# Token norms by sums in four column groups and products with a selector, with a new order of the first stage

## The chip, the cores and the metric

The kernel runs on one core of a Trainium2 chip. The core has five engines that run side by side: TensorE multiplies matrices (PE in the profile, and PEld for its loads of the stationary operand), VectorE (DVE), ScalarE (ACT) and GpSimd (POOL) work elementwise, and SyncE (SP) issues most of the transfers between the chip's main memory and the on-chip memory. Each engine has a queue and takes its instructions in the order of that queue; an instruction that waits holds up all that stand behind it. A matmul writes to tiles in a memory called PSUM.

The metric is the device time in microseconds (us) of one execution, the median of several runs.

## The reference

1024 tokens of 1024 channels go through two layers. Each layer begins with an RMS norm over the channels, scaled and shifted by vectors that come from a vector c (for 256 context tokens in the first layer, from c_ctx):

```python
def rmsnorm(x, g):
    xf = x.astype(jnp.float32)
    y = xf * lax.rsqrt(jnp.mean(xf * xf, axis=-1, keepdims=True) + RMS_EPS)
    return (y * g.astype(jnp.float32)).astype(x.dtype)
...
    for l in range(DEPTH):
        shift, scale, gate = jnp.split(sc @ mod_w[l] + mod_b[l], 3, axis=-1)
        hx = modulate(rmsnorm(x, norm_g[l]), shift[:, None], scale[:, None])
        if ctx_out_needed or l % 2 == 0:
            hc = modulate(rmsnorm(ctx, norm_g[l]), shift_c, scale_c)
        ...
        x = x + gate[:, None] * out_x
    return rmsnorm(x, final_g)
```

The first layer projects h to the parts va, vg, ga, xb and gb. The parts va and vg go through a sigmoid gate and a convolution of 31 taps, xb through a short convolution and a linear recurrence in both directions, and the result is projected back. The recurrence has a decay for each channel that comes from a parameter vector lam:

```python
    log_a = -LRU_C * r * jax.nn.softplus(-p["lam"].astype(jnp.float32))
    a = jnp.exp(log_a)
    bx = jnp.sqrt(-jnp.expm1(2.0 * log_a)) * (i * uf)
```

The second layer projects h to u and g, takes u less its windowed means, multiplies with one weight matrix for each of four groups, gates and projects back.

## The kernel before

All data lie with channels on the 128 partitions and tokens along the free axis, so x is eight tiles of 128 x 1024. A product of two fp32 matrices is made of three matmuls on split operands: each operand is cast to a shorter format (`fp32r`) on ScalarE, and the rest is taken by a subtraction on VectorE or GpSimd (`split`). The names carry `h` and `l` for the two parts (`wh_`, `wl_`, `h0h`, `h0l`); `wr_` is the weight as loaded. A product is three matmuls.

The "folds" multiply two weights of the second layer with each other ahead of their use: group g's weight `gh`/`gl` (from `graw`) with four blocks `wh_wu_g_kp`. Each block gives two accumulations of 12 matmuls, `fold_g_kp_0` and `fold_g_kp_1`, whose results are copied out (`fo`) and stored. Folds 0 and 1 run in the first stage, folds 2 and 3 near the end of the first layer. They fill TensorE while the norms and the modulation are being worked out.

**First stage (some 67 us).** Fourteen matmuls on constants (`warm`) start the span. Then `fold(0)` and `fold(1)` run, and beside them x is loaded, squared on ScalarE and summed over its eight tiles on VectorE (`ssq`, two halves of 512 tokens). What remains is a sum over 128 partitions. `rstd_cols` takes it by four matmuls of one column for each half (`ms_x<-ones,ssq`), a square root (`rc`) and a reciprocal on 128 x 4 numbers, a diagonal matrix `dg` made of them and the identity `idx`, and one plain fp32 matmul of `ones` with `dg` (`roots`), which spreads the factor of each token over all partitions. The modulation of x comes from four blocks of c times `modW`: `modr_b` is 16 matmuls of 32 columns each in four column groups of the array, `modrow_b` their copy on ScalarE, and `modt_b` four tiny matmuls that turn it to a column. VectorE scales x by the factor of its token (`x<-x,a,ms_x`), ScalarE makes `h0h` and VectorE `h0l`. The first projection then starts: xb, vg, va and the gates of the recurrence, with the context (`cx`, `xbc`) between them. Six "gates" (`mod<-mod,cL`, 128 x 1024) reduce rows of `modT` with the activated c_ctx (`cL`) for the context.

`decay_rates` works out the decay's constants `chalf` and `cneg` from lam by some twenty small VectorE instructions between two folds of the first stage.

**What sets the order.** In the first stage the order of matmuls is the order of the code, chained one to the next by `mm`, and the order of loads and stores on SP's queue likewise by `load`; `fold_some(n)` takes n steps of the folds, `store_folds(n)` issues n stores. The instructions of the other engines are put in order by a scheduler that goes by the code's order, by dependences and by explicit `issue_after`. From the first projection on (`chained[0] = False`) a second planner in the same program orders them.

**The second norm** (n1, near 757 to 770 us) is the same `rstd_cols` on two halves, while folds 2 and 3 run on TensorE; its factors scale `x1` (`x<-x,a,ms_n`, 16 instructions), and the split x feeds the quads of the second layer (`qa_v`, `qc_v`, ...).

## Time and profile before

| | us |
|---|---|
| median of 3 runs | 1286.2 (1284.6 to 1286.56) |
| the profiled execution | 1282.57 |
| its span | 1280.8 |
| PE busy | 1261.2 |
| DVE busy | 1136.8 |
| ACT busy | 654.6 |
| POOL busy | 290.2 |

The span runs from the first to the last instruction that the profiler recorded, so 1.8 us of the execution lie around it. A row of a timeline gives the start and the length of an instruction or of a run of like ones, the engine, the line of the code, the operation, the tiles that it writes and reads with their numbers left out, and in brackets the idle time ahead of it with what ended it. The length of a matmul includes its way through the array, so consecutive matmuls overlap: the pace is the distance of their starts.

### The profile page before, as it was taken

The page shows a single profiled execution, that of the slowest core. Times are in us where ns is not written, and L with a number is a line of the kernel's source. Part 1 is how long each engine was busy: PE and PEld are TensorE (multiplying, and loading weights), DVE is VectorE, ACT ScalarE, POOL GpSimd, SP SyncE. Part 2 cuts the span into 40 slices and gives each one's busy share as a digit, 9 for nine tenths or more (in the row PEclk, how much of TensorE's full clock was granted, in tenths as well). Part 3 has the DMA queues.
Part 4 walks back from the last instruction along what each step waited for, and adds up shares of the span by engine and source line. Part 5 has one row for each costly group of instructions (what it writes and reads, how often), then busy time and mean ns, then how long its engine had stood idle before and what let it go on. Part 6 is the DMA issues. An engine that isn't in the chain of part 4 may idle for free.

```text
span 1280.8 us, 16137 instructions
## 1 busy us (share of the span) xinstructions
PE 1261.2 (98%) x5824; PEld 1041.3 (81%) x5824; DVE 1136.8 (89%) x1765; ACT 654.6 (51%) x954; POOL 290.2 (23%) x147
## 2 busy tenths in 40 slices
...
PEclk9999999999999999999999999999999999999998
...
GB/s 373 396 219 50 42 75 41 66 42 75 42 82 42 82 124 135 154 140 83 164 49 288 175 214 180 91 130 151 122 98 134 115 123 132 303 227 286 212 105 132
DMA packets 78847, 182.33 MB, mean 142 GB/s; under 512 B 7728, under 2 KB 23472, under 8 KB 78768
## 3 DMA queue, kind: packets, MB, share of 16 engines
...
## 4 chain that ended last, share of the span: by engine, by line
PE 57%; DVE 24%; DMA 10%; issue 4%; ACT 2%; POOL 2%; SPq 0%; POOLq 0%; DVEq 0%; ACTq 0%
PE wob L553 7%; PE vg L553 5%; PE va L553 5%; DVE conv L553 5%; PE xb L553 4%; PE fold L123 3%; DVE l L553 3%; PE g L553 3%; PE ga L553 2%; PE ga L144 2%; PE ga L145 2%; PE gb L553 2%; PE ga L146 2%; DMA yr_t<-y_t 2%; PE xbc L553 2%
## 5 line engine op out<-in xcount | busy, mean ns | idle before, releaser
L553 DVE SCALAR_TENSOR_TENSOR conv<-u,sm,conv 128x505 f32<-128x505 f32 (+6 forms) x224 | 153.7, 746 | 1.0
L1658 POOL TENSOR_TENSOR o<-x,rr 128x256 f32<-128x256 f32 (+1 forms) x10 | 9.7, 1004 | 445.7 <-ACT rr L1658 443.5
L553 ACT ACTIVATE l<-g,sm 128x512 f32<-128x512 f32 (+1 forms) x96 | 58.7, 619 | 57.8 <-PE g L553 57.0
L103 ACT CAST wq_g<-wr_g 128x512 fp32r<-128x512 f32 x48 | 28.2, 620 | 55.5 <-DVE wr_g L998 23.0
L553 POOL TENSOR_TENSOR l<-l,l 128x1280 f32<-128x1280 f32 x16 | 47.1, 2968 | 25.6 <-DVE conv L553 14.1
L123 PE MATMUL fold<-gh,wh_wu 128*128 128x512 f32 x128 | 51.1, 400 | 1.4 <-ACT wh_wu L103 1.4
L123 PE MATMUL fold<-gh,wl_wu 128*128 128x512 f32 x128 | 50.2, 395 | 0.1
L553 PE MATMUL gb<-h0h,wl_gb 128*128 128x512 f32 x128 | 49.9, 390 | 0.3 <-POOL wl_gb L553 0.3
L123 PE MATMUL fold<-gl,wh_wu 128*128 128x512 f32 x128 | 50.1, 392 | 0.0
L553 PE MATMUL va<-h0h,wl_va 128*128 128x512 f32 x128 | 50.0, 390 | 0.1
L553 PE MATMUL vg<-h0h,wl_vg 128*128 128x512 f32 x128 | 49.9, 390 | 0.0
L553 PE MATMUL gb<-h0h,wh_gb 128*128 128x512 f32 x128 | 49.9, 390 | 0.0
L553 PE MATMUL gb<-h0l,wh_gb 128*128 128x512 f32 x128 | 49.9, 390 | 0.0
L553 PE MATMUL va<-h0l,wh_va 128*128 128x512 f32 x128 | 49.9, 389 | 0.0
L553 PE MATMUL va<-h0h,wh_va 128*128 128x512 f32 x128 | 49.8, 389 | 0.0
L553 PE MATMUL vg<-h0h,wh_vg 128*128 128x512 f32 x128 | 49.8, 389 | 0.0
L553 PE MATMUL wob<-ybl,wh_wob 128*128 128x512 f32 x128 | 49.8, 389 | 0.0
L553 PE MATMUL wob<-ybh,wh_wob 128*128 128x512 f32 x128 | 49.8, 389 | 0.0
L553 PE MATMUL wob<-ybh,wl_wob 128*128 128x512 f32 x128 | 49.8, 389 | 0.0
L553 PE MATMUL vg<-h0l,wh_vg 128*128 128x512 f32 x128 | 49.8, 389 | 0.0
L553 DVE TENSOR_TENSOR_SCAN l<-l,l 128x256 f32<-128x256 f32 (+1 forms) x32 | 48.7, 1521 | 1.1
L553 DVE SCALAR_TENSOR_TENSOR conv<-cL,wsum,conv 128x506 f32<-128x506 f32 (+3 forms) x70 | 48.2, 746 | 0.2
...
## 6 DMA issues: line engine op xcount, KB each, us to landing
...
```

Of the source, the lines that this page charges most:

```text
L103: return (nc.scalar.copy(hi, src), eng.tensor_tensor(out=lo, in0=src, in1=hi.bitcast(F32), op=sub))
L123: m = nc.tensor.matmul(*args, **kw)
L144: mm(ps, hi[:, kc], xh[k][:, cols], start=(k == 0), stop=False)
L145: mm(ps, hi[:, kc], xl[k][:, cols], start=False, stop=False)
L146: mm(ps, lo[:, kc], xh[k][:, cols], start=False, stop=(k == ks - 1))
L553: last[eng] = f(*args, **kw)
L1658: tail[eng] = f(*args, **kw)
```

## The change

The edits go together under four heads.

1. **The norms.** `rstd_cols` is gone, and with it the identity in the first stage. `rstd_pair` takes both halves at once: eight matmuls of 32 output rows and 128 columns, spread over the four column groups of the array, write the sums to one tile of 128 x 256; one square root, one reciprocal, a cast (`hi`) and a subtraction (`lo`) follow on that tile; eight matmuls with a `selector` (zeros, with one row of ones for each group) spread the factors over the partitions.
2. **The first fold.** The first tile of `graw` and the first fold weight are loaded and split in halves, in an order of products that takes the first halves first (`first_terms`).
3. **The order of the first stage.** The loads of `modW` are apart from their products and stand earlier, the products are interleaved with folds in steps (`fold_part` takes a piece of a fold), stores stand later, there is one more buffer for them, the activations of c and c_ctx have other places, and all six gates stand behind the split of the context.
4. **The decay constants** are worked out on GpSimd, but for one reciprocal on VectorE, in the first projection.

```diff
-    def decay_rates():
+    def decay_exp():
         nc.scalar.activation(sa, lam, AF.Abs)
         nc.scalar.activation(sa, sa, AF.Exp, scale=-1.0)
-        nc.vector.tensor_scalar(out=sb, in0=sa, scalar1=2.0, scalar2=None, op0=add)
-        nc.vector.reciprocal(sb, sb)
-        nc.vector.tensor_tensor(out=sz, in0=sa, in1=sb, op=mult)
-        nc.vector.tensor_tensor(out=sb, in0=sz, in1=sz, op=mult)
-        nc.vector.memset(sa, 1.0 / 17.0)
+
+    def decay_rates():
+        scaled = lambda o, x, c, op: on("pool", nc.gpsimd.tensor_scalar, out=o, in0=x, scalar1=c, scalar2=None, op0=op)
+        scaled(sb, sa, 2.0, add)
+        vec(nc.vector.reciprocal, out=sb, in_=sb)
+        gp(out=sz, in0=sa, in1=sb, op=mult)
...
-    def rstd_cols(acc, name, idD, rpool, wn):
-        n = acc.shape[-1]
-        nt = n // P
-        ps, root = banks(f"ms_{name}", wn)
-        r = rpool.tile([P, H // P], F32, tag="rc", name=f"rc_{name}")[:, :nt]
-        for c in range(nt):
-            mm(ps[:, c : c + 1], acc[:, c * P : (c + 1) * P], ones[:, 0:1], start=True, stop=True)
-        nc.scalar.activation(r, ps[:, :nt], AF.Sqrt, bias=eps_r)
-        nc.vector.reciprocal(r, r)
-        t = ttile(f"dg_{name}")[:, :n]
-        nc.vector.tensor_tensor(out=t.rearrange("p (c t) -> p c t", t=P),
-                                in0=idD.unsqueeze(1).to_broadcast([P, nt, P]),
-                                in1=r.unsqueeze(2).to_broadcast([P, nt, P]), op=mult)
-        roots = lambda: mm(root[:, :n], ones, t, start=True, stop=True)
-        if not chained[0]:
-            roots()
-        return root[:, :n], roots
+        return act
+
+
+    def selector(name):
+        sel = tpool.tile([P, H], F32R, tag="t", name=f"sel_{name}")
+        nc.vector.memset(sel.bitcast(F32), 0.0)
+        for e in range(4):
+            nc.vector.memset(sel[32 * e : 32 * e + 1, e * P : (e + 1) * P].bitcast(F32), 1.0)
+        return sel
+
+
+    def rstd_pair(accs, name, sel, ps, root):
+        v = ttile(f"sq_{name}")[:, : 2 * P]
+        pair = tpool.tile([P, H], F32R, tag="t", name=f"hl_{name}")
+        hi, lo = pair[:, : 2 * P], pair[:, 2 * P :]
+        for q in range(2):
+            for e in range(4):
+                c = (2 * e + q) % 4 * P
+                mm(ps[32 * e : 32 * e + 32, q * P : (q + 1) * P], ones[:, :32], accs[e // 2][:, c : c + P],
+                   start=True, stop=True, skip_group_check=True)
+        nc.scalar.activation(v, ps[:, : 2 * P], AF.Sqrt, bias=eps_r)
+        nc.vector.reciprocal(v, v)
+        nc.vector.tensor_copy(out=hi, in_=v)
+        nc.vector.tensor_tensor(out=lo, in0=v, in1=hi.bitcast(F32), op=sub)
+
+        def roots():
+            for e in range(4):
+                for i, x in enumerate((hi, lo)):
+                    mm(root(e), sel[:, e * P : (e + 1) * P], x, start=(i == 0), stop=(i == 1))
+        return roots
...
+            for h in HALF:
+                load(graw[0][:, h], grp[g, 0][:, h])
+                load(wraw[:, h], wu[g, 0][:, h])
+            load(graw[1], grp[g, 1])
+            for h in HALF:
+                for raw, hi, lo in ((graw[0], ghs[0], gls[0]), (wraw, *early)):
+                    split(raw[:, h], hi[:, h], lo[:, h], nc.vector)
+            split(graw[1], ghs[1], gls[1], nc.vector)
...
-        def mod_loads(b, qs):
-            if b not in modr:
-                modr[b] = psum(f"modr_{b}")
-            for q in qs:
-                raw = dtile(f"modw_{b}_{q}") if b < 3 else ctile(f"modw_{b}_{q}", F32)
-                load(raw, modW[b, q])
+        modraw = {}
+
+        def mod_loads(b):
+            for q in range(4):
+                modraw[b, q] = dtile(f"modw_{b}_{q}") if b < 3 else ctile(f"modw_{b}_{q}", F32)
+                load(modraw[b, q], modW[b, q])
+
+        def mod_products(b):
+            modr[b] = psum(f"modr_{b}")
+            for q in range(4):
+                raw = modraw[b, q]
...
-            nc.scalar.activation(cL, cL, AF.Silu)
...
-            rstd(accc, eps_r, "c")
+            with tc.issue_after(rstd(accc, eps_r, "c").ins):
+                nc.scalar.activation(cL, cL, AF.Silu)
...
-        load(idx, ident)
         load(ccv, ccol)
-        nc.scalar.activation(cpad[:, :, 0:2], ccv, AF.Silu)
         load(sm, small)
-        fold_some(2)
-        decay_rates()
+        fold_some(3)
+        for k in range(5, 8):
+            last_square = x_load(k)
+        with tc.issue_after(last_square.ins):
+            silu_c = nc.scalar.activation(cpad[:, :, 0:2], ccv, AF.Silu)
+        with tc.issue_after(silu_c.ins):
+            nc.scalar.activation(a1[:, 0, 0:1], eps_r, AF.Sqrt)
+        mod_loads(0)
         fold_some(1)
-        for k in range(5, 8):
-            x_load(k)
         store_folds(1)
-        fold_some(3)
-        rx = [rstd_cols(acc[h][:, :H], f"x{h}", idx, spool, h) for h in range(2)]
-        mod_loads(0, range(4))
-        for _, roots in rx:
-            roots()
-        rx = [r for r, _ in rx]
+        mod_loads(1)
+        fold_some(1)
+        rx = banks("rx", 0)
+        roots = rstd_pair([acc[h][:, :H] for h in range(2)], "x", sel_x, wide("ms_x"),
+                          lambda e: rx[e // 2][:, (e % 2) * 2 * P : (e % 2 + 1) * 2 * P])
+        fold_some(1)
+        mod_products(0)
         mod_row(0)
+        roots()
         mod_cols(0)
         modulate(0)
         modulate(1)
-        mod_loads(1, range(4))
+        mod_loads(2)
+        fold_some(2)
+        mod_products(1)
         mod_row(1)
-        store_folds(2)
-        fold_some(2)
+        fold_part(1)
         mod_cols(1)
+        fold_some(1)
         modulate(2)
         modulate(3)
+        store_folds(1)
+        mod_loads(3)
         fold_some(1)
-        mod_loads(2, range(4))
+        mod_products(2)
         mod_row(2)
+        fold_part(1)
+        mod_cols(2)
+        fold_some(1)
+        fold_part(2)
         store_folds(1)
-        fold_some(2)
-        mod_cols(2)
-        mod_loads(3, range(4))
+        mod_products(3)
         with tc.issue_after(mod_row(3).ins):
             modulate(4)
         modulate(5)
+        fold_part(1)
+        mod_cols(3)
         fold_some(1)
-        mod_cols(3)
         modulate(6)
         last_low = modulate(7)
         w_xb0 = wload(win[3 * KT], "xb0", nc.vector)
-        store_folds(1)
         fold_some(2)
         with tc.issue_after(last_low[0].ins), tc.issue_after(last_low[1].ins):
             ctx_load(0)
-            squares = ctx_load(1)
+            ctx_load(1)
+        store_folds(2)
         w_vg0 = wload(win[KT], "vg0", nc.vector)
         store_folds(2)
         spread_c()
-        with tc.issue_after(squares.ins):
-            gates(2 * KT, 2 * KT + 2)
         raw_va0 = wpool.tile([P, D], F32, tag="wr", name="wr_va0")
         load(raw_va0, win[0])
         store_folds(1)
@@ -538,8 +599,10 @@
         for _ in first:
             pass
         ctx_split(0)
-        with tc.issue_after(ctx_split(1)[1].ins):
-            gates(2 * KT + 2, 2 * KT + 6)
+        high, low = ctx_split(1)
+        with tc.issue_after(high.ins), tc.issue_after(low.ins):
+            decay_exp()
+            gates(2 * KT, 2 * KT + 6)
...
+    wide_n = wide("rs")
+    with tc.issue_after(squared[0].ins), tc.high_priority(offset=EVAC):
+        nc.scalar.activation(dsh[:, 0:1], eps_r, AF.Sqrt)
+        roots = rstd_pair([nacc[h][:, :H] for h in range(2)], "n1", selector("n1"), banks("ms_n1", 0)[0],
+                          lambda e: wide_n[:, 2 * e * P : 2 * (e + 1) * P])
+    roots()
+    rs = [wide_n[:, h] for h in HALF]
     nc.vector.tensor_tensor(out=dsh, in0=m1[:, 0, KH:KT], in1=m1[:, 0, 0:KH], op=sub)
-    rs = [rstd_cols(nacc[h][:, :H], f"n1{h}", idD, hpool, h)[0] for h in range(2)]
```

Three places show how the order of an engine's instructions moves. The numbers behind a name tell tiles of the same name apart.

ScalarE before, in the middle of the first stage: `modrow` is the copy of a block of the modulation, `wh_wu_2` the cast of fold 1's third weight, `h0h` a split of x, `fo` a fold's copy.

```order
L390 COPY modrow_520<-modr_493 128x512
L411 ACTIVATE h0h_533<-x_227,m_132 128x1024
L411 ACTIVATE h0h_539<-x_231,m_132 128x1024
L390 COPY modrow_568<-modr_543 128x512
L103 CAST wh_wu_2_574<-wr_wu_2_572 128x1024
L302 COPY fo_1_580<-fold_1_0_578 128x4x128
L411 ACTIVATE h0h_605<-x_274,m_132 128x1024
L302 COPY fo_1_580<-fold_1_1_579 128x4x128
L411 ACTIVATE h0h_611<-x_282,m_132 128x1024
L390 COPY modrow_653<-modr_628 128x512
L103 CAST wh_wu_3_658<-wr_wu_3_656 128x1024
L302 COPY fo_2_664<-fold_2_0_662 128x4x128
```

ScalarE now, at the same place:

```order
L440 COPY modrow_505<-modr_488 128x512
L461 ACTIVATE h0h_526<-x_238,m_132 128x1024
L343 COPY fo_1_552<-fold_1_0_550 128x4x128
L461 ACTIVATE h0h_532<-x_242,m_132 128x1024
L440 COPY modrow_583<-modr_566 128x512
L461 ACTIVATE h0h_609<-x_285,m_132 128x1024
L343 COPY fo_1_552<-fold_1_1_551 128x4x128
L461 ACTIVATE h0h_615<-x_293,m_132 128x1024
L440 COPY modrow_651<-modr_634 128x512
L103 CAST wh_wu_2_546<-wr_wu_2_544 128x1024
L103 CAST wh_wu_3_630<-wr_wu_3_628 128x1024
```

The cast of `wh_wu_2` stood behind the second `modrow` and ahead of the second pair of `h0h`; it now stands behind the third `modrow`, and directly ahead of the cast of `wh_wu_3`. The matmuls of `fold_1_2_0`, the first that read it, follow the 16 matmuls of `modr_2` on TensorE in both orders.

VectorE before, from the last sum of the context's squares to the first product of the gated convolution (`u`), with the repeated rows between them left out:

```order
L365 TENSOR_TENSOR ssqc<-ssqc,csq_3_823 128x256
L446 SCALAR_TENSOR_TENSOR mod_16_836,m_132<-mod_16_836,cL 128x1024
L446 SCALAR_TENSOR_TENSOR mod_17_839,m_132<-mod_17_839,cL 128x1024
L204 RECIPROCAL ssqc<-sq_c 128x256
...
L104 TENSOR_TENSOR ctl_812<-cx_810,cth_811 128x1024
L446 SCALAR_TENSOR_TENSOR mod_18_913,m_132<-mod_18_913,cL 128x1024
...
L446 SCALAR_TENSOR_TENSOR mod_21_922,m_132<-mod_21_922,cL 128x1024
L553 SCALAR_TENSOR_TENSOR uc_948<-xb_845,sm,uc_948 128x1022
...
L553 SCALAR_TENSOR_TENSOR l_946,m_132<-l_946,cL 128x1024
L553 TENSOR_TENSOR m_132<-m_132,sm 128x8
L553 TENSOR_TENSOR u_1060<-va_0_1061,sg_0_983 128x512
```

VectorE now:

```order
L410 TENSOR_TENSOR ssqc<-ssqc,csq_3_806 128x256
L208 RECIPROCAL ssqc<-sq_c 128x256
...
L104 TENSOR_TENSOR ctl_795<-cx_793,cth_794 128x1024
L496 SCALAR_TENSOR_TENSOR mod_16_894,m_132<-mod_16_894,cL 128x1024
L496 SCALAR_TENSOR_TENSOR mod_17_897,m_132<-mod_17_897,cL 128x1024
L496 SCALAR_TENSOR_TENSOR mod_18_900,m_132<-mod_18_900,cL 128x1024
...
L496 SCALAR_TENSOR_TENSOR mod_21_909,m_132<-mod_21_909,cL 128x1024
L616 SCALAR_TENSOR_TENSOR uc_935<-xb_823,sm,uc_935 128x1022
...
L616 SCALAR_TENSOR_TENSOR l_933,m_132<-l_933,cL 128x1024
L616 TENSOR_TENSOR m_132<-m_132,sm 128x8
L616 RECIPROCAL sb<-sb 128x16
L616 TENSOR_TENSOR u_1074<-va_0_1075,sg_0_970 128x512
```

The first two gates stood ahead of the reciprocal of the context's norm and now stand behind the context's split, and the reciprocal of the decay constants stands ahead of `u`.

TensorE before, at the second norm: the first of the two groups of column sums for one half (the rows of `ms_n` with `ones` and `n1acc`), and the two products that spread the factors.

```order
L123 MATMUL fold_0_1_6369<-gh_1_6304,wh_wu_0_6310 128x512
L123 MATMUL ms_n_6285<-ones,n1acc_5639 128x1 x4
L123 MATMUL fold_0_1_6369<-gl_1_6305,wh_wu_0_6310 128x512
...
L123 MATMUL ms_n_1_6274<-dg_n_6282,ones 128x512
L123 MATMUL fold_2_1_6433<-gh_0_6298,wl_wu_2_6323 128x512
L123 MATMUL fold_2_1_6433<-gh_0_6298,wh_wu_2_6322 128x512
L123 MATMUL fold_2_1_6433<-gl_0_6299,wh_wu_2_6322 128x512
L123 MATMUL fold_2_1_6433<-gh_0_6298,wl_wu_2_6323 128x512
L123 MATMUL ms_n_6285<-dg_n_6293,ones 128x512
```

TensorE now, the sums and the products with the selector:

```order
L123 MATMUL fold_1_1_6424<-gl_0_6322,wh_wu_1_6339 128x512
L123 MATMUL ms_n_0_6294<-n1acc_5652,ones 32x128 x2
L123 MATMUL ms_n_0_6294<-n1acc_5653,ones 32x128 x2
...
L123 MATMUL fold_3_0_6487<-gh_0_6321,wl_wu_3_6352 128x512
L123 MATMUL fold_3_0_6487<-gh_0_6321,wh_wu_3_6351 128x512
L123 MATMUL rs<-hl_n_6297,sel_n_6288 128x256
L123 MATMUL fold_3_0_6487<-gl_0_6322,wh_wu_3_6351 128x512
L123 MATMUL fold_3_0_6487<-gh_0_6321,wl_wu_3_6352 128x512
L123 MATMUL rs<-hl_n_6297,sel_n_6288 128x256 x7
L123 MATMUL fold_3_0_6487<-gh_1_6327,wh_wu_3_6351 128x512
```

The sums, which the four column groups now share, stand in the second accumulation of the second block instead of the first block (and the start of the second), and the products that spread the factors from the second accumulation of the third block (`fold_2_1`) to the first accumulation of the fourth (`fold_3_0`).

75 lines of the change are left out of this document (51 added, 24 removed).

## The prediction

> **What bounds the kernel now.** I read the page first, then TensorE's waits, then the timelines of the first 130 us and of the second norm. The page:
>
> ```profile
> span 1280.8 us, 16137 instructions
> ...
> PE 1261.2 (98%) x5824; PEld 1041.3 (81%) x5824; DVE 1136.8 (89%) x1765; ACT 654.6 (51%) x954; POOL 290.2 (23%) x147
> ...
> PEclk9999999999999999999999999999999999999998
> ```
>
> TensorE is busy in 98% of the span and its clock is granted nearly in full everywhere. So the time can move in two ways only: TensorE gets fewer or cheaper matmuls, or it waits more or less. TensorE's waits, us in total, times and longest:
>
> ```profile
> PE fold L123 <- ACT wh_wu L103: 1.4, 1, 1.4
> ...
> PE gb L553 <- POOL wl_gb L553: 0.3, 1, 0.3
> ```
>
> Asked for 8 to 130 us alone, this view has no row. A first stage without waits has nothing to give but its own matmuls, and whatever is made late there shows at once. The rest of the change must be costed by what it takes from or adds to TensorE's queue, and by the waits that it makes.
>
> **The norms on TensorE.** The first stage, TensorE's timeline (start, length):
>
> ```profile
> 7.05 0.58 PE L123 MATMUL fold<-gh,wh_wu 128*128 128x512 f32 x1
> 7.46 0.40 PE L123 MATMUL fold<-gl,wh_wu 128*128 128x512 f32 x1
> 7.98 0.50 PE L123 MATMUL fold<-gh,wl_wu 128*128 128x512 f32 x1
> ...
> 35.18 1.84 PE L123 MATMUL ms_x<-ones,ssq 128*128 128x1 f32 x16
> 36.95 1.93 PE L123 MATMUL modr<-modw,cpad 128*32 128x256 f32 x32
> 38.81 2.20 PE L123 MATMUL ms_x<-dg_x,ones 128*128 128x512 f32 x4
> 40.85 0.95 PE L123 MATMUL modt<-sm,modrow 128*128 128x2 f32 x8
> ...
> 52.44 0.50 PE L123 MATMUL fold<-gh,wh_wu 128*128 128x512 f32 x1
> 52.77 0.40 PE L123 MATMUL fold<-gl,wh_wu 128*128 128x512 f32 x1
> ```
>
> and the same engine in the chain of work that ended last (start, length, count):
>
> ```profile
> 61.83 5.61 PE fold L123 x24
> 67.44 8.16 PE xb L123 x36
> ...
> 89.67 2.89 PE xbc L553 x24
> ```
>
> By the distance of starts, the old sums of x cost 36.95 - 35.18 = 1.77 us and the old products 40.85 - 38.81 = 2.04, together 3.8. A plain fp32 matmul is two records here. The trace has no sums in four column groups, but `modr` is a product in four groups: 32 records of 256 columns take 38.81 - 36.95 = 1.86, so 0.058 each. The new sums are 16 records of 128 columns. At half of 0.058 they cost 0.46; at the pace of the old one-column records (1.77 / 16 = 0.11) they would cost 1.77, no gain. I take 0.7, near the low end, because `modr` has the same shape of operand, plus what a change of shape costs: behind `modr` the first fold's matmul takes 52.77 - 52.44 = 0.33 instead of the folds' pace of 5.61 / 24 = 0.23, so 0.1 on each side. The new products are eight of 256 columns, as `xbc` has them at 2.89 / 24 = 0.12: together 0.95. So a norm costs 1.65 instead of 3.8 and TensorE is spared 2.1 us (1.0 to 2.4), in each of two norms. The Trainium skill, page "TensorEngine Tiling (Array Packing)", section "Tiling Modes", speaks against this: a change of the tiling mode drains the array. Taken as one whole matmul lost (0.39) on each side of the sums, the norm's gain would be 1.5 instead of 2.1; the 0.33 behind `modr` shows about 0.1 a switch, so I keep 2.1.
>
> **The first fold.** The matmul at 7.98 came 0.52 after its predecessor and not 0.23: it waited for the rest of the first weight. With halves that wait goes, 0.3 us. The start at 7.05 stays, since the warm-up matmuls end just ahead of it. Gain 0.3 (0 to 0.5).
>
> **The first stage's new waits.** ScalarE's timeline there:
>
> ```profile
> 46.12 0.56 ACT L390 COPY modrow<-modr 128x512 f32<-128x512 f32 x1
> 46.58 1.04 ACT L103 CAST wh_wu<-wr_wu 128x1024 fp32r<-128x1024 f32 x1
> ...
> 50.70 1.15 ACT L411 ACTIVATE h0h<-x,m 128x1024 fp32r<-128x1024 f32 x1 [2.59 <-DVE x L408]
> ...
> 53.28 0.57 ACT L390 COPY modrow<-modr 128x512 f32<-128x512 f32 x1
> 53.74 1.05 ACT L103 CAST wh_wu<-wr_wu 128x1024 fp32r<-128x1024 f32 x1
> ```
>
> The cast at 46.58 is that of `wh_wu_2`; its first reader is the fold's matmul at 52.44, six us later, and nothing waits. In the new order this cast stands behind the third `modrow`, which waits for the last matmul of `modr_2`; the fold that reads it stands directly behind `modr_2` on TensorE. So TensorE must wait from the end of `modr_2` for the copy and the cast: 53.74 - 53.28 = 0.46 until the cast begins, 1.05 for the cast, and some 0.25 for two handovers, 1.75 in all. Two matmuls on (0.46) stands the first reader of `wl_wu_2`, which VectorE subtracts only after the cast:
>
> ```profile
> 62.38 1.22 DVE L104 TENSOR_TENSOR wl_xb<-wr_xb,wh_xb 128x1024 fp32r<-128x1024 f32 x1
> ```
>
> 1.22 less 0.46 is another 0.75. The fourth `h0h` (1.15) stands ahead of that `modrow` and may push it by up to 0.6. New wait: 2.5 us (2.3 to 3.1), certain by the order alone. SP's queue is held too: the load of `wr_xb0` waits for this `wl_wu_2`, and the context's tiles and `wr_vg0` stand behind it.
>
> Two smaller waits come with it. The sums now stand two accumulations (24 matmuls, 5.5 us) earlier against the last squares of x, some 0.25. The products wait for the chain square root, reciprocal, cast, subtraction on 128 x 256, against two shorter ones on 128 x 4 before; its dearest part is the reciprocal, whose row is that of the context's norm:
>
> ```profile
> 76.97 1.75 DVE L204 RECIPROCAL ssqc<-sq_c 128x256 f32<-128x256 f32 x1
> ```
>
> With 0.45 for the root, 1.75, and about 0.4 each for cast and subtraction (a third to a half of a 1.22) the chain takes 3.2 with handovers, and twelve matmuls and `modr_0` (2.75 + 1.86 = 4.6) stand between sums and products. ScalarE has the last squares and two table loads ahead of the root, so I leave 0.5 for it (0 to 1). First stage: -2.1 - 0.3 + 2.5 + 0.25 + 0.5 = +0.8. From that I take 0.5 because the pieces of modulation stand up to 2 us earlier and their small waits ahead of `modt` go with it: **+0.3** (-0.8 to +1.7). No load was removed but the identity; what moves is their order, and cover for a late load is thin: `h0h_7` now stands behind the cast of `wh_vg0`.
>
> **Gates and decay constants.** VectorE around 90 us, and TensorE behind it:
>
> ```profile
> 89.41 1.22 DVE L446 SCALAR_TENSOR_TENSOR mod<-mod,cL 128x1024 f32<-128x1024 f32 x1
> ...
> 91.72 3.92 DVE L553 SCALAR_TENSOR_TENSOR uc<-xb,sm,uc 128x1022 f32<-128x1022 f32 x3 [1.08 <-ACT uc L553]
> ...
> 105.51 1.27 DVE L553 TENSOR_TENSOR u<-va,sg 128x512 f32<-128x512 f32 x2
> ```
>
> ```profile
> 107.62 0.40 PE L553 MATMUL g<-uh,wh_gw 128*128 128x512 f32 x1
> ```
>
> Two gates that stood ahead of the reciprocal, where VectorE waited for the context's root, now stand behind the context's split: 2 x 1.2 = 2.4 more ahead of `uc`, of which its wait of 1.08 takes a part. So `uc`, and with it `u`, comes 1.3 later, and the reciprocal of the decay's constants, waiting for GpSimd behind `wl_gw`, adds 0.2 to 0.7. The first of the two `u` ends at 105.51 + 0.64 = 106.15 now, and at 107.6 to 108.1 then. The second `g` needs the PSUM tile that this `u` reads free, at 107.62 (+0.3). I take **+0.3** (0 to 1). Further on the delay is absorbed: VectorE's waits from 85 to 320 us are
>
> ```profile
> DVE uc L553 <- ACT uc L553: 5.7, 9, 1.1
> DVE u L553 <- PE va L553: 2.9, 4, 0.9
> ```
>
> 8.6 us, all on results that follow TensorE's own pace. The 22 small instructions taken from VectorE in the first stage hid under folds and give nothing. On GpSimd 25 of them now stand between the end of `wl_gw`, 121.99 - 16.43 = 105.56, and `wl_vg`, which TensorE reads first at 124.86:
>
> ```profile
> 121.99 2.41 POOL L553 TENSOR_TENSOR wl_vg<-wr_vg,wh_vg 128x1024 fp32r<-128x1024 f32 x1 [16.43 <-ACT wh_vg L553]
> ```
>
> ```profile
> 124.86 0.39 PE L553 MATMUL vg<-h0h,wl_vg 128*128 128x512 f32 x1
> ```
>
> The prices of GpSimd's nearest rows (total, then mean ns of one):
>
> ```profile
> L1658 POOL TENSOR_TENSOR o<-x,rr 128x256 f32<-128x256 f32 x6 | 4.2, 724 | 3.4 <-issue 2.2 <-ACT rr L1658 1.2
> L1507 POOL MEMSET vp<- 128x64 f32 x4 | 0.6, 152 | 0.0
> ```
>
> At 0.152 they take 4 us, at 0.724 18 us; they have 16 columns, so I take the low row, and they end near 112, in the idle 16.43 us. "GPSIMD Engine Reference" of the Trainium skill (section "Key points") adds that GpSimd shares its interfaces to on-chip memory with VectorE, which would slow the convolution beside them; at 4 us of small instructions that would be a few tenths on an engine with the slack above. Cost 0.
>
> **The second norm.** TensorE, then VectorE:
>
> ```profile
> 757.58 0.95 PE L123 MATMUL ms_n<-ones,n1acc 128*128 128x1 f32 x8
> 768.75 1.02 PE L123 MATMUL ms_n<-dg_n,ones 128*128 128x512 f32 x2
> ```
>
> ```profile
> 769.81 10.62 DVE L1376 SCALAR_TENSOR_TENSOR x<-x,a,ms_n 128x512 f32<-128x512 f32 x16 [2.24 <-PE ms_n L123]
> ...
> 785.48 0.69 DVE L997 TENSOR_TENSOR ws_v<-wr_v,wr_v 128x512 f32<-128x512 f32 x1 [0.40 <-DMA wr_v<-wfold]
> ...
> 803.97 0.70 DVE L104 TENSOR_TENSOR x_t1l<-x,x_t1h 128x512 fp32r<-128x512 f32 x1
> ```
>
> ```profile
> 804.75 0.39 PE L1018 MATMUL qc_v<-x_t1h,wq_v 128*128 128x512 f32 x1
> ```
>
> TensorE saves about 2.1 here too (the sums for the other half and the other product have rows of the same lengths). But the first product moves 14 matmuls on (3.2 us of folds, less what TensorE gains), and the first scaling needs the last of eight products instead of the first of two: I put it at 771.6 instead of 769.81. VectorE then has no idle time to 804 but the 0.40 at 785.48, so its splits come 1.4 later, while TensorE comes to them 2.1 earlier. The last `x_t1l` is done at 804.67 and read by the matmul behind the one at 804.75, so there is about 0.1 to spare. TensorE waits there and at the next splits, and what is left of 2.1 is 2.1 - 1.5 = 0.6: **-0.6** (-2.1 to +1.4, the lower end if VectorE starts no later than now, the upper if its whole delay reaches TensorE).
>
> **The sum.** +0.3 + 0.3 - 0.6 = 0.0. The profiled execution took 1282.57 and stays there; it lies 3.6 below the median of the runs, 1286.2. I predict 1286 for the median, no change. A measurement of this kernel tells about 0.2% (2.6 us) from no change.
>
> **The rivals.**
> - *Both norms keep their gain.* Products with the selector arrive at VectorE by 769.8, and in the first stage the 0.5 and 0.25 of small waits don't show: -2.1 - 0.3 + 2.5 - 0.5 = -0.4, gates 0, n1 -2.1, and squares and loads that no longer collide give up to 1 more: -3.5, 1282.7. For it: sums and products are sure to be cheaper, and VectorE has 2.24 idle ahead of the scaling. Against it: the order of the products.
> - *The held queue makes the first projection wait* (the other sign). `wr_xb0`, the context and `wr_vg0` are issued only once `wl_wu_2` is done, near 53.4; `wh_vg0` stands ahead of `h0h_7` on ScalarE, and `h0h_7` is read 21 matmuls after the first projection starts. With 0.4 to 1 us to spare there, a landing of `wr_vg0` more than 1 us later than I place it decides; 3 us late gives +2 here, with the +1.7 of the first stage +3.7: 1290. Against it: the first reader of `wr_vg0` on TensorE comes only after `xb`, 11 us behind its start at 67.44.
> - *GpSimd's small instructions are dear.* They may take 14 us before `wl_vg` at 121.99 is pushed and TensorE's first reader (124.86) with it, that is 0.57 each. At 0.724 they take 18: +3.5, 1289.7. Against it: the 0.152 row.
> - *The column groups don't overlap*, the sums cost 1.77 as before in both norms: +2.1, and the sums' delay of about 1 reaches VectorE in n1: 1289.
>
> **The numbers.** No change 0.37, both norms keep their gain 0.32, the held queue 0.17, column groups 0.09, GpSimd 0.05. Thus faster 0.32, within 0.2% 0.37, slower 0.31. The likeliest case alone spans 1283.6 to 1288.8. The bounds of the terms add up to -2.9 and +4.1, and with the two larger rivals the range is 1281 to 1291.
>
> **What would show it.** TensorE's waits should have a new row, `fold` on ScalarE's `wh_wu` or VectorE's `wl_wu`, of 2 to 3 us near 50; if it is missing, the first stage's sum is wrong. `ms_x` in four groups should take less than 1 us. `xb` should start between 66.7 and 69 (now 67.4). VectorE's `x<-x,a,rs` should start near 771.6 on the old clock, and TensorE should wait for `x_t1l` or `x_t2l` near 804. GpSimd's last small instruction should end ahead of 116. A wait on `h0h`, `wl_vg` or `g` of more than 1 us would make the prediction wrong upward.

## The result: 0.4% slower

| | before | after |
|---|---|---|
| median, us | 1285.79 (4 runs) | 1292.23 (4 runs, 1291.76 to 1292.71) |
| ratio, 95% interval | | 1.0043 (1.0026 to 1.0060) |
| profiled execution, us | 1282.57 | 1291.87 |
| its span, us | 1280.8 | 1289.8 |

1286.0 was predicted, with a range of 1281 to 1291. The ratio is +5.5 us (3.3 to 7.7); it is not the quotient of the two medians, which lie 6.4 us apart. The two traced executions lie 9.3 apart, since that of before took 3.2 less than its median: of the differences between the two traces below, some 3 us do not belong to the change. The page after:

```profile
span 1289.8 us, 16163 instructions
...
PE 1263.5 (98%) x5832; PEld 1039.7 (81%) x5832; DVE 1139.0 (88%) x1750; ACT 654.7 (51%) x955; POOL 297.0 (23%) x173
...
PEclk9899999999999999999999999999999999999998
```

TensorE's clock, full before in every slice but the last, is down in the second one (32 to 64 us). Before, TensorE had no wait from 8 to 130 us. Its waits from 0 to 130 us now (total, times, longest; `warm` was there before, too):

```profile
PE fold L123 <- ACT wh_wu L103: 2.0, 1, 2.0
PE xbc L616 <- POOL wl_xb L616: 1.6, 1, 1.6
PE warm L123 <- DVE ones L161: 1.1, 1, 1.1
PE va L616 <- POOL wl_va L616: 0.7, 1, 0.7
PE fold L123 <- DVE gl L104: 0.5, 1, 0.5
PE fold L123 <- DVE wl_wu L104: 0.5, 1, 0.5
PE ms_x L123 <- DVE ssq L410: 0.2, 1, 0.2
```

The table locates the loss: it gives the start of the first matmul of a few products on TensorE (us), from the timelines of before, of a second trace of the same kernel, of the changed kernel, and of the main experiments, which are told below. `qa_woa` ends the first layer, `qa_v` and `qa_g` are the first products of two groups of the second (the time from one to the other is called the v group), and `fin_ms` belongs to the last norm.

| | `xb` | `g` | `qa_woa` | `qa_v` | `qa_g` | `fin_ms` |
|---|---|---|---|---|---|---|
| before | 67.3 | 106.6 | 671.7 | 800.0 | 812.4 | 1256.2 |
| before, second trace | 67.4 | 106.7 | 671.9 | 800.8 | 813.4 | 1257.6 |
| after | 72.6 | 114.3 | 679.5 | 805.7 | 822.1 | 1265.2 |
| filler | 68.8 | 110.6 | 675.8 | 804.2 | 820.8 | 1266.1 |
| weights early | 66.2 | 108.0 | 673.1 | 800.5 | 816.3 | 1260.2 |
| gate behind | 69.8 | 109.7 | 674.7 | 802.5 | 818.2 | 1264.4 |
| both | 65.3 | 105.2 | 670.3 | 797.8 | 815.4 | 1258.5 |
| both, old second norm | 66.1 | 106.0 | 671.0 | 800.0 | 812.5 | 1258.1 |
| the same, old first fold | 65.3 | 105.2 | 670.2 | 798.7 | 813.9 | 1259.7 |
| new second norm alone | 67.4 | 106.7 | 672.0 | 799.3 | 815.0 | 1260.9 |

After is 5.3 us late at `xb`, 7.7 at `g`, and 7.8 at `qa_woa`: nothing happens between 115 and 670 us. At `qa_v` it is 5.7 late, so the second norm gives 2 us; at `qa_g` it is 9.7 late again: the v group takes 16.4 us instead of 12.4. Three places are to be explained.

**First stage.** TensorE's timeline after:

```profile
33.07 0.41 PE L123 MATMUL ms_x<-ssq,ones 128*32 128x128 f32 x4
33.67 0.63 PE L123 MATMUL ms_x<-ssq,ones 128*32 128x128 f32 x12 [0.19 <-DVE ssq L410]
...
39.06 1.21 PE L123 MATMUL rx<-hl_x,sel_x 128*128 128x256 f32 x8
...
53.64 0.50 PE L123 MATMUL fold<-gh,wh_wu 128*128 128x512 f32 x1 [2.05 <-ACT wh_wu L103]
...
54.90 0.79 PE L123 MATMUL fold<-gh,wl_wu 128*128 128x512 f32 x1 [0.53 <-DVE wl_wu L104]
55.49 1.70 PE L123 MATMUL modt<-sm,modrow 128*128 128x2 f32 x8
...
57.62 0.63 PE L123 MATMUL fold<-gl,wh_wu 128*128 128x512 f32 x1
58.05 0.63 PE L123 MATMUL fold<-gh,wl_wu 128*128 128x512 f32 x1
```

The sums and products are about as cheap as forecast, and the wait on `wh_wu_2` and `wl_wu_2` stands where the prediction put it: 2.05 + 0.53 = 2.6 us. But behind it the folds take 0.63 each at a distance of 0.43, not 0.39 and 0.23. The view by stretches shows why (stretch, length, busy time of PE, PEld, DVE, ACT, POOL, then the clock granted to TensorE, the transfers' share and GB/s). After:

```profile
54.00:56.00 2.00, 1.47 (x7) 1.00 (x5) 0.84 (x1) 1.05 (x1) 0.00 (x0) 0.71 0.43 144
56.00:58.00 2.00, 2.00 (x8) 1.86 (x9) 0.74 (x5) 0.00 (x0) 0.00 (x0) 0.50 0.77 262
58.00:60.00 2.00, 2.00 (x6) 1.56 (x5) 2.00 (x4) 0.00 (x0) 0.00 (x0) 0.50 0.96 278
60.00:62.00 2.00, 2.00 (x6) 1.56 (x6) 1.55 (x2) 0.58 (x1) 0.00 (x0) 0.58 0.94 290
```

Before, at the same place:

```profile
56.00:58.00 2.00, 2.00 (x35) 1.09 (x34) 1.75 (x7) 0.07 (x1) 0.00 (x0) 1.00 1.07 385
```

For some 6.5 us, 55 to 61.5, TensorE runs at half its clock. That is worth about 2.9 us: 0.20 more for each of eleven fold matmuls, and 1.70 for `modt` instead of 0.95. The Trainium skill, "TensorE: Matmul & The Clock Gate", Part 1, describes such a gate, with a window of 3.4 us of idleness ahead of the half clock. The measurement differs from the page: a wait of 2.05 us and one of 0.53, with two matmuls between, were enough here.

The trace of before has such a place too, at its very end. With waits of 0.92 us (up to 1266.95) and 1.76 (up to 1271.88) its clock is 0.55 from 1270 to 1272 and 0.50 after, and the second of two like products takes 1.19 instead of 0.68. TensorE's timeline before:

```profile
1269.03 0.68 PE L1658 MATMUL fin_ms<-dg,ones 128*128 128x256 f32 x2
1271.88 1.19 PE L1658 MATMUL fin_ms<-dg,ones 128*128 128x256 f32 x2 [1.76 <-DVE dg L1658]
```

**Gates.** VectorE's timeline after:

```profile
95.51 1.22 DVE L496 SCALAR_TENSOR_TENSOR mod<-mod,cL 128x1024 f32<-128x1024 f32 x1
...
96.66 3.40 DVE L496 SCALAR_TENSOR_TENSOR mod<-mod,cL 128x1024 f32<-128x1024 f32 x1
...
100.00 3.91 DVE L616 SCALAR_TENSOR_TENSOR uc<-xb,sm,uc 128x1022 f32<-128x1022 f32 x3
```

GpSimd's, after:

```profile
95.97 3.01 POOL L616 TENSOR_TENSOR wl_va<-wr_va,wh_va 128x1024 fp32r<-128x1024 f32 x1 [95.53 <-ACT wh_va L616]
108.19 3.36 POOL L616 TENSOR_TENSOR wl_xb<-wr_xb,wh_xb 128x1024 fp32r<-128x1024 f32 x1 [9.21 <-ACT wh_xb L616]
...
113.75 0.26 POOL L616 TENSOR_SCALAR sb<-sa 128x16 f32<-128x16 f32 x1
114.39 0.22 POOL L616 TENSOR_TENSOR sz<-sa,sb 128x16 f32<-128x16 f32 x1 [0.37 <-DVE sb L616]
```

The sixth gate takes 3.40 us instead of 1.22, while GpSimd subtracts `wl_va` (3.01). The trace of before already had such a pair a little later, a VectorE product over the gate's shape, beside `wl_xb` on GpSimd:

```profile
100.99 3.41 DVE L553 SCALAR_TENSOR_TENSOR l<-l,cL 128x1024 f32<-128x1024 f32 x1
```

```profile
99.92 3.41 POOL L553 TENSOR_TENSOR wl_xb<-wr_xb,wh_xb 128x1024 fp32r<-128x1024 f32 x1 [6.85 <-ACT wh_xb L553]
```

The lengths fit with two engines that take turns: `wl_va` ends at 98.98 and the gate that began at 96.66 ends 1.08 later; `l` of before ends 1.07 behind `wl_xb`. No run tests that by itself.

So `uc` starts at 100.00 (91.72 before), which is 27.4 us behind the start of `xb` instead of 24.4, and ScalarE, whose queue holds the cast of `uc` ahead of that of the weight `wh_xb`, brings the weight late: TensorE waits 1.6 for `wl_xb`. The small instructions of the decay constants cost 0.1 to 0.3 each (one 0.65), and TensorE waits for none of them.

**Second norm.** VectorE's timeline after:

```profile
773.29 1.75 DVE L230 RECIPROCAL sq_n<-sq_n 128x256 f32<-128x256 f32 x1
775.62 1.22 DVE L104 TENSOR_TENSOR gl<-graw,gh 128x1024 fp32r<-128x1024 f32 x1 [0.58 <-ACT gh L103]
776.76 0.28 DVE L231 CAST hl_n<-sq_n 128x256 fp32r<-128x256 f32 x1
777.08 0.43 DVE L232 TENSOR_TENSOR hl_n<-sq_n,hl_n 128x256 fp32r<-128x256 f32 x1
780.08 10.62 DVE L1447 SCALAR_TENSOR_TENSOR x<-x,a,rs 128x512 f32<-128x512 f32 x16 [2.57 <-PE rs L123]
```

The scaling stands 2.4 us later against `qa_woa` than before (100.6 us behind its start, 98.1 before and 98.8 in the second trace of before), for the products of the selector: VectorE has the chain done at 777.5 and then waits for TensorE's turn.

### The profile page after: what moved, and what is told of

It is laid out like the page before. It is cut to its first block, busy times and chain, and to the rows that moved or that the text cites. A ratio compares the mean times of both kernels' runs of the same rounds, so it can differ in the third digit from the quotient of the medians.

```text
span 1289.8 us, 16163 instructions
## 1 busy us (share of the span) xinstructions
PE 1263.5 (98%) x5832; PEld 1039.7 (81%) x5832; DVE 1139.0 (88%) x1750; ACT 654.7 (51%) x955; POOL 297.0 (23%) x173
## 4 chain that ended last, share of the span: by engine, by line
PE 59%; DVE 21%; DMA 12%; issue 3%; POOL 2%; ACT 2%; SPq 0%; POOLq 0%; DVEq 0%; ACTq 0%
PE wob L616 7%; DVE conv L616 5%; PE xb L616 4%; PE va L616 4%; PE vg L616 4%; DVE l L616 3%; PE g L616 3%; DMA wr_wu<-wu 2%; DMA modw<-modW 2%; PE ga L616 2%; PE ga L145 2%; PE ga L144 2%; PE gb L616 2%; PE ga L146 2%; PE qb_v L1084 2%
```

## The experiments

"Late" and "early" are against the kernel before unless another is named. Each but the filler, which ran once, has its ratio to runs of the kernel before on the same chip.

### The first stage

*Weight earlier.* One load moved, so that `wu_1_2` is fetched ahead of the third block of `modW`:

```diff
         roots()
+        fold_some(2)
         mod_loads(2)
-        fold_some(2)
```

> The changed kernel with one edit: fold 1's third weight is loaded ahead of the four modW loads of block 2, so that its cast stands behind the second modrow again. Theory (the wait for this cast, 2.05 + 0.53 us, and the half clock that follows it, some 2.9 us, make the 5.35 us by which xb starts late): both waits go, the folds behind them run at 0.23 us and not 0.43, xb starts at 67.3 to 67.8 instead of 72.79, and the time falls by 5.4 us, to 1286.8. Rival (TensorE waits there anyway, for modW or the next weight, which now land later): xb starts at 70 or later and the time falls by 2.5 us at most.

1290.89 us, ratio 1.0062 (1.0040 to 1.0083), `xb` at 71.3. The wait on `wh_wu_2` went, but two of 1.0 came in its place (`modt` on `modrow`, near 54, and a fold on `wl_wu`, near 66), and the clock was down again from 54 to 58 us, to 0.61 and 0.54. It missed because it made another hole at the same place.

*Filler.* Nine matmuls of `ones` with itself into a tile that nobody reads, ahead of the fold that waits. They lie inside the wait, which stays.

```diff
         mod_products(2)
+        filler = psum("filler")
+        for _ in range(9):
+            mm(filler[:, :P], ones, ones, start=True, stop=True)
         mod_row(2)
```

> The changed kernel with nine plain matmuls of ones (128 columns) put between modr_2 and the fold that waits for the cast; their result is not used. They fill the wait of 2.05 us with work and shorten nothing. Theory (the half clock is a consequence of TensorE standing idle): the clock of 0.50 from 56 to 60 us is gone, the folds behind run at 0.23 us, and xb starts near 69.9, 2.9 earlier than in the changed kernel though the cast comes no earlier. Rival (the low clock has another cause, the load of the chip at this time): the clock falls all the same and xb starts at 72.8 or later.

The stretch that ran at half clock:

```profile
56.00:58.00 2.00, 2.00 (x10) 1.66 (x9) 2.00 (x5) 0.25 (x1) 0.00 (x0) 1.00 0.83 252
```

The clock is 1.00 throughout, and `xb` starts at 68.8 instead of 72.6, `g` at 110.6 instead of 114.3. The fold that waits for the cast starts 20.6 us behind the first sum of the norm, as in after, so nothing but the clock was changed: the half clock is what the idle TensorE brought on itself.

What it costs can be read from four kernels with this first stage, from the first sum of the norm to `xb`. It takes 39.6 us in after and in the run with the old second norm (told below), whose clock is down for 6.8 us by the trace's record; 38.0 in the run with one gate behind (below), where the same two waits leave the clock down for 3.4 us; and 36.3 with the filler. So the fall cost half of its length, 3.2 us in after, and how long it lasts was not the same from run to run. The time of the single filler run, 1292.49, does not show the gain: `fin_ms` is at 1266.1, and the gain has gone behind 675 us.

*Both weights early.* The loads of `wu_1_2` and `wu_1_3` ahead of the third and fourth block, and the fourth `h0h` behind `modrow_2` on ScalarE:

```diff
+        fold_some(2)
         mod_loads(2)
-        fold_some(2)
...
         modulate(2)
-        modulate(3)
         store_folds(1)
-        mod_loads(3)
         fold_some(1)
+        mod_loads(3)
         mod_products(2)
-        mod_row(2)
+        with tc.issue_after(mod_row(2).ins):
+            modulate(3)
```

> The changed kernel with the third and the fourth weight of fold 1 loaded ahead of the modW loads of their blocks, and the third modrow ahead of the fourth h0h on ScalarE, so that neither cast nor that modrow stands behind something TensorE must finish first. Theory (each cast that stands behind a modrow makes TensorE wait, and the pauses bring the half clock): no wait of TensorE over 0.6 us between 8 and 70 us, the clock stays at 1.00, xb starts at 66.8 to 67.8, and the time falls by 5.0 us from the changed kernel's. Rival (the rest of the new order cannot be fed by the transfers): the wait appears once more at another tile, xb starts at 69 or later.

1287.89, ratio 1.0020 (1.0004 to 1.0036). The waits on `wh_wu` and `wl_wu` are gone, the clock is full in this stage, and `xb` starts at 66.2, 1.1 earlier than in the kernel before. From the first sum to `xb` it takes 33.5 us, 2.8 less than with the filler: that is the price of the waits themselves. Against before the loss falls from 5.5 us to 2.6, where 0.5 was expected; the two intervals (3.3 to 7.7 and 0.5 to 4.6) overlap, so it is the traces that show this gain. The norm's saving on TensorE is seen to be real in this stage.

### The gates

*Two gates back* ahead of the context's reciprocal, with the activation of `cL`:

```diff
             load(cL, cc[0].partition_broadcast(P))
+            nc.scalar.activation(cL, cL, AF.Silu)
...
-            with tc.issue_after(rstd(accc, eps_r, "c").ins):
-                nc.scalar.activation(cL, cL, AF.Silu)
+            rstd(accc, eps_r, "c")
...
+        with tc.issue_after(squares.ins):
+            gates(2 * KT, 2 * KT + 2)
...
-            gates(2 * KT, 2 * KT + 6)
+            gates(2 * KT + 2, 2 * KT + 6)
```

> The changed kernel with two of the six gates, and the activation of c_ctx that they need, back where they stood before. Theory (the two gates make uc 2.4 us late, behind it stands the cast of the next xb weight on ScalarE, and TensorE waits 1.6 us for wl_xb and 0.7 for wl_va): both waits go, the first g follows the start of xb by 39.1 us as before (41.7 in the changed kernel), and the time falls by 2.3 us. Rival (the lateness of VectorE comes from the late start of the first projection or from the decay constants): the waits stay and the time is within 0.7 us of the changed kernel's.

1296.87, ratio 1.0088 (1.0062 to 1.0114). The wait on `wl_xb` went, but in the changed order of the first stage the gates delay the context's norm (`ms_c` waits 2.7 for `ssqc`). Besides the fall near 60 us the clock fell to 0.50 at 14 to 16 us, behind the first fold's wait for its second halves. Undoing a part in its old place can cost more than the part.

*One gate behind.* The sixth gate stands behind the subtraction `ul`, where VectorE no longer holds up `uc`:

```diff
-            gates(2 * KT, 2 * KT + 6)
+            gates(2 * KT, 2 * KT + 5)
...
-            vec(nc.vector.tensor_tensor, out=ul, ...)
+            ulop = vec(nc.vector.tensor_tensor, out=ul, ...)
...
             if state is None:
+                with tc.issue_after(ulop.ins):
+                    gates(2 * KT + 5, 2 * KT + 6)
```

> The changed kernel with the sixth gate moved from ahead of uc to behind ul. Theory (this gate runs while GpSimd subtracts wl_va, and both read two operands from the on-chip memory: it took 3.40 us instead of 1.22, and held uc, uh, the cast of wh_xb and with it wl_xb): five gates end before wl_va starts, uc starts 3 us earlier against the start of vg (12.9 us behind it, now 15.8), the waits for wl_xb (1.6) and wl_va (0.7) go, and the time falls by 2.3 us. Rival (uc collides with wl_va instead, or the sixth gate collides with wl_xb and holds u): the first g comes less than 1 us earlier, and the time falls by less than 1.

VectorE's timeline there:

```profile
102.31 1.22 DVE L496 SCALAR_TENSOR_TENSOR mod<-mod,cL 128x1024 f32<-128x1024 f32 x1
...
103.46 3.41 DVE L616 SCALAR_TENSOR_TENSOR l<-l,cL 128x1024 f32<-128x1024 f32 x1
```

1290.95, ratio 1.0045 (1.0030 to 1.0060). The gate takes 1.22 again, and it is `l`, which now runs beside `wl_xb`, that takes 3.41, as before the change. The wait on `wl_xb` is gone. From `xb` to `g` it takes 39.9 us: 39.3 in the kernel before and in the run with the new second norm alone, 41.7 to 41.8 in all runs with the changed gates but for the gates put back, 39.9 in all with the sixth gate behind. So the late gate cost 1.8 at `g`, and 0.6 stays, which fits the wait on `wl_va` (0.7). The time shows none of it: 2.3 us less were expected, and the ratio is that of the changed kernel. That `xb` stands 2.8 ahead of after's is not the gate's doing: the norm's sums came 1.3 earlier, and the clock was down for half as long.

*Both*, weights early and gate behind:

> The edits of the two kernels above together. If the theories hold, all that the changed kernel loses in the first 130 us is regained (xb at 67.3, first g at 105.5 to 106.5), and what is left is the gain of the second norm: 1 to 2 us faster than the kernel before. If the second norm's gain is lost behind it, the time is that of the kernel before within 1 us.

1287.91, ratio 1.0020 (1.0005 to 1.0035). `xb` is 2.0 and `g` 1.4 earlier than before, more than the theory had, and `qa_v` 2.2 earlier; but `qa_g` is 3.0 late, and instead of 1 to 2 us faster the kernel is 2.6 slower than before. What is left is behind the second norm.

### The second norm

*Old norm.* The changed kernel with the second norm of before:

```diff
-    wide_n = wide("rs")
-    with tc.issue_after(squared[0].ins), tc.high_priority(offset=EVAC):
-        nc.scalar.activation(dsh[:, 0:1], eps_r, AF.Sqrt)
-        roots = rstd_pair([nacc[h][:, :H] for h in range(2)], "n1", ...)
-    roots()
-    rs = [wide_n[:, h] for h in HALF]
+    rs = [rstd_cols(nacc[h][:, :H], f"n1{h}", idD, hpool, h)[0] for h in range(2)]
```

> The changed kernel with the second norm as before (column sums for each half, diagonal matrices). Theory (the new second norm gives TensorE 2.0 us at first and takes 3.9 back, since VectorE starts the scaling 2.5 us later than the shift of the stage): the v products begin 2.0 later than in the changed kernel, the waits for qb_v and wq_g (0.9 and 1.1) go, and the time falls by 1.9 us. Rival (what is lost behind the second norm comes from loads that arrive late whatever the norm): the waits stay and the time rises by 2.0 us.

1291.14, ratio 1.0062 (1.0038 to 1.0085). `qa_v` comes later (809.4), `qa_g` where it was (822.1): the norm's gain on TensorE had bought nothing. The waits for `qb_v` and `wq_g` are gone, as expected, but the time did not fall by 1.9; it lies above the changed kernel's, by less than the runs can tell.

*New norm alone* in the kernel before, the same lines the other way round:

> The kernel before with the new second norm (n1) alone: sums by four column groups, selector's products, the Sqrt table ahead; nothing of the first stage or of the gates is changed. Theory: TensorE starts the v group 2 us earlier but the scaling starts about 2.5 us later, so the v group takes 15 to 17 us instead of 12.5 and the time is 0.5 to 2.5 us above before. Rival A: the norm's saving on TensorE is kept, 2 us below before. Rival B: both cancel, within 0.5 us of before.

1287.33, ratio 1.0023 (1.0012 to 1.0035), so +3.0 us. VectorE's timeline:

```profile
765.32 1.75 DVE L225 RECIPROCAL sq_n<-sq_n 128x256 f32<-128x256 f32 x1
767.88 1.22 DVE L104 TENSOR_TENSOR gl<-graw,gh 128x1024 fp32r<-128x1024 f32 x1 [0.82 <-ACT gh L103]
...
773.67 1.41 DVE L1412 SCALAR_TENSOR_TENSOR x<-x,a,rs 128x512 f32<-128x512 f32 x2 [3.90 <-PE rs L123]
```

The sums stand later too. TensorE's timeline before, and then with the new norm alone:

```profile
760.34 0.95 PE L123 MATMUL ms_n<-ones,n1acc 128*128 128x1 f32 x8
```

```profile
762.71 0.64 PE L123 MATMUL ms_n<-n1acc,ones 128*32 128x128 f32 x16
```

The scaling starts 3.9 us later than before (769.81). It is the place of the products in TensorE's queue that decides: VectorE has the chain done at 769.8 and waits 3.90 for them. ScalarE's first cast for the v group, `x_b11h`, comes 3.2 later than its 779.37 too. TensorE's largest wait in the v group, 1.1 us at `qa_g`, is for ScalarE's cast of `wq_g`, which stands behind `x_t4h`, and that waits for VectorE. ScalarE's timeline before, and then with the new norm alone:

```profile
811.20 0.62 ACT L103 CAST x_t4h<-x 128x512 fp32r<-128x512 f32 x1 [4.98 <-DVE x L966]
```

```profile
813.81 0.62 ACT L103 CAST x_t4h<-x 128x512 fp32r<-128x512 f32 x1 [5.12 <-DVE x L995]
814.33 0.61 ACT L103 CAST wq_g<-wr_g 128x512 fp32r<-128x512 f32 x1
```

*Fixes with the old norm.* Both fixes, and the second norm of before:

> The changed kernel with the two weight loads of the first stage ahead of the modulation blocks, the sixth gate behind the `ul` subtraction, and the second norm (n1) as the kernel before computes it; the first norm, the first fold's halves and the decay constants stay as changed. Theory (three separate costs: late weight, late gates, and a scaling that starts later behind the new second norm): the first projection still starts 2.0 us earlier than before, the first product of `g` 1.4 earlier, and with the old norm the v group takes its 12.5 us again, so the time is 1283 to 1285 where before gives 1285. Rival A (the loss behind 675 us is a matter of how the loads fall and not of the norm): the v group still takes 15 us or more and the time is 1287 to 1288, as with both fixes alone.

1285.23, ratio 1.0006 (0.9993 to 1.0018). The v group takes its 12.5 us again and the time is that of before. `xb` and `g` start 1.2 and 0.5 earlier than before, not 2.0 and 1.4, and that does not show in the time.

*Old first fold.* The same, with the loads and the order of the first fold of before:

> As the kernel with the two fixes and the old second norm, with the first fold of the kernel before: whole loads and splits of its inputs and the old order of its first 48 matmuls. Theory (the halves cost, because the second halves land 0.4 us too late for the new order): the square sums of the first norm start up to 0.6 us earlier and the time falls by 0.3 to 0.6 us against the kernel with halves. Rival (the halves gain 0.3 us as the prediction had it): 0.3 us later.

1283.87, ratio 0.9998 (0.9983 to 1.0013). The times alone do not separate it from the kernel with halves, but the traces do. With halves and early weights `xb` starts at 66.2, 65.3, 66.1 and 66.0 in four kernels, without at 65.3, 65.1, 65.2 and 65.4. The halves cost some 0.6 us instead of gaining 0.3. The first fold starts up to 1 us earlier with them (5.6 to 6.3 against 6.6 to 6.9 in these kernels) and gives that back in waits for the second halves, as in the trace of after, TensorE's timeline:

```profile
10.13 0.73 PE L123 MATMUL fold<-gh,wh_wu 128*128 128x512 f32 x2
11.39 0.50 PE L123 MATMUL fold<-gl,wh_wu 128*128 128x512 f32 x1 [0.53 <-DVE gl L104]
```

The sums of the norm then start about when they do without halves, but with halves they wait for `ssq` and take 1.16 us to the next fold, without 0.58: there the 0.6 arises.

One reading stands against the late scaling as the only cause. In the trace of this kernel, with the old norm and the scaling only 98.3 us behind `qa_woa`, the v group takes 15.2 us as well, with two waits on `x_t1l` (2.1 in all); its `x_b11h` comes 110.4 behind `qa_woa`, 107.7 before. So one trace's v group is not the norm's doing alone.

*Delay, too small.* On top of the fixes with the old norm, a reciprocal, a copy and a product on a tile of ones on VectorE ahead of the scaling:

```diff
+    more = ttile("more")[:, : 2 * P]
+    nc.vector.memset(more, 1.0)
+    for _ in range(1):
+        nc.vector.reciprocal(more, more)
+        nc.vector.tensor_copy(out=more, in_=more)
+        nc.vector.tensor_tensor(out=more, in0=more, in1=more, op=mult)
```

> As the kernel with the two fixes and the old second norm, with three more VectorE instructions on a tile of ones between the old norm's diagonal products and the scaling of x: a reciprocal, a copy and a product of 128x256, which is what the new norm puts there (1.75, 0.28 and 0.43 us, together 2.5 us). Nothing else is changed. Theory (VectorE is full from 770 to 829 us and TensorE waits for its scaled x): the v group becomes 2 to 2.5 us longer and so does the time. Rival (the delay is hidden, and what costs is the new norm's order of the scaling or its PSUM banks): the v group stays at 12.5 us and the time does not change by more than 0.5 us.

1284.63, ratio 1.0012 (0.9995 to 1.0029), like the kernel without it. It settled nothing: the three ran in time in which VectorE would have waited, and the scaling started at 769.75.

*Delay, held.* The same with three reciprocals, on the kernel with the old first fold, and a product of the scale `a1` with ones at the end, so that the scaling cannot pass it:

```diff
+    for _ in range(1):
+        nc.vector.reciprocal(more, more)
+        nc.vector.reciprocal(more, more)
+        nc.vector.reciprocal(more, more)
...
+    nc.vector.tensor_tensor(out=a1[:, 0, :], in0=a1[:, 0, :], in1=more[:, :KT], op=mult)
```

> The two fixes, the first fold of before and the old second norm, with three reciprocals, a copy and a product of 128x256 on a tile of ones and a product of the scale by ones in VectorE's queue right ahead of the scaling, so that the scaling starts 3.5 to 4.5 us later. Theory: the v group becomes 2 to 4 us longer and the time is 2 to 4 us above the same kernel without the delay, 1286 to 1288. Rival: the delay is hidden and the time stays at 1284.

VectorE's timeline:

```profile
769.19 1.75 DVE L1411 RECIPROCAL more<-more 128x256 f32<-128x256 f32 x1
770.98 2.32 DVE L1412 COPY more<-more 128x256 f32<-128x256 f32 x1
...
774.07 1.40 DVE L1446 SCALAR_TENSOR_TENSOR x<-x,a,ms_n 128x512 f32<-128x512 f32 x2
```

1288.75, ratio 1.0026 (1.0013 to 1.0039). With the old norm and a scaling that starts 104.1 us behind `qa_woa` instead of 98.3, the time is 3.6 us above the kernel without the delay (1.0026 against 0.9998; the intervals touch at 1.0013). So a late scaling is enough to cost what the new norm costs, by the medians. The traced executions, 1285.11 and 1285.95, do not show the 3.6; in them the v group takes 16.8 us against 15.2, and TensorE waits 1.1 for `wq_g` at `qa_g`, as with the new norm alone.

*Norm drawn together.* The reverse: the new norm, with its products 24 instead of 40 fold matmuls behind the sums, and both splits of the last fold (`gl`) behind the norm's low part on VectorE. First with the two fixes and the old first fold, then alone in the kernel before:

```diff
+                        if chain_end[1] is not None and (g, kp, s) in [(2, 2, 1)]:
+                            fctx.enter_context(tc.issue_after(chain_end[1].ins))
                         for _ in terms(s):
...
-    for f in (fold2, fold2, fold3, fold3):
-        next(f)
+    next(fold2)
+    next(fold2)
+    with tc.issue_after(chain_end[0].ins):
+        next(fold3)
+    next(fold3)
```

> The two fixes and the first fold of the kernel before, with the new second norm, whose chain is drawn together: the low part on VectorE ahead of the first split of the last fold, and the eight selector's products 24 instead of 40 fold matmuls behind the sums. Theory (the late start of the scaling is what costs): the scaling starts within 1 us of where the kernel with the old norm starts it (about 769.5), the 2 us that the norm spares TensorE are kept, and the time is 1 to 2 us below that of the kernel with the two fixes, the first fold of before and the old second norm, so 1282 to 1283. Rival (the new norm costs by its order or its PSUM banks): 2 to 3 us above it, 1286 to 1287.

> The kernel before with the new second norm alone, drawn together in the same way (the low part ahead of the first split of the last fold, the products 24 instead of 40 fold matmuls behind the sums). Theory: the 3 us that the new norm alone cost are gone, and the time is 0 to 2 us below before. Rival: it stays 2 to 3 us above before.

1289.69, ratio 1.0039 (1.0020 to 1.0057), and 1291.4, ratio 1.0048 (1.0034 to 1.0063): worse than the new norm as it was, by both theories a miss. The scaling did start early (770.3 and 771.3), but the last fold's weights are cast late, after waits for their loads of up to 3.9 and 5.7 us, and `x_b11h`, behind them in ScalarE's queue, starts at 784.0 and 786.9. VectorE stands idle for 3.8 and 5.8 us between. That the held splits delay these loads, by keeping `graw`, is argued and not shown. In both traces TensorE's clock falls to 0.50 as well, in the first near 752 and 810 us, in the second near 715 and from 807 to 817.5.

*Early on both sides.* Only the second of those splits is held, and the Sqrt table load of 1.28 us, which the change had put ahead of a weight cast on ScalarE, is left where the Sqrt stands. Again with the fixes and alone:

```diff
-        nc.scalar.activation(dsh[:, 0:1], eps_r, AF.Sqrt)
...
+                if chain_end[0] is not None and (g, i) == (3, 1):
+                    gctx.enter_context(tc.issue_after(chain_end[0].ins))
                 split(raw, th, tl, nc.vector)
```

> The two fixes, the first fold of before and the new second norm with its products 24 instead of 40 fold matmuls behind the sums, only the second split of the last fold behind the norm's low part, and no Sqrt table load put ahead (it comes where the Sqrt itself stands). Theory (two gates side by side, the scaling on VectorE and the fold's casts on ScalarE): scaling starts at 769 to 770.5, the first cast for the v group at 778 to 780.5, the v group takes 12 to 13.5 us, and the norm's 2 us on TensorE are kept: 1282 to 1284. Rival (the loads of the fold's weights run later whatever the order, since TensorE gets there 2 us earlier): the cast stays at 782 or later and the time at 1286 to 1289.

> The kernel before with that second norm alone. Theory: 0 to 2 us below before. Rival: 2 to 4 us above it.

1285.7, ratio 1.0004 (0.9991 to 1.0018), and 1286.84, ratio 1.0010 (0.9999 to 1.0022). Alone, the scaling now starts at 768.65, but `x_b11h` only at 781.66, ScalarE's timeline:

```profile
780.71 1.05 ACT L103 CAST wh_wu<-wr_wu 128x1024 fp32r<-128x1024 f32 x1 [1.66 <-DMA wr_wu<-wu]
781.66 2.56 ACT L1415 ACTIVATE x_b11h<-x,m 128x512 fp32r<-128x512 f32 x4
```

and TensorE, which is 1.6 us ahead at `qa_v`, gives that back. Its largest wait from 790 to 830 us, and the stretch behind it:

```profile
PE qc_v L1058 <- DVE x_t1l L104: 2.2, 1, 2.2
```

```profile
808.00:810.00 2.00, 2.00 (x6) 1.56 (x5) 2.00 (x4) 0.00 (x0) 0.00 (x0) 0.50 0.78 289
```

The kernel before has no wait of TensorE from 790 to 830 us, and its clock is full there. Here TensorE is at half clock behind the waits, from 805.7 to 812.5, as in the trace with the fixes (804.7 to 811.5). This trace, of the norm alone, is of the slowest of twelve executions (1291.65), so it does not stand for the median. By the medians 1.7 of the 3.0 us came back, which is less than the runs can tell, and nothing of what the norm spares TensorE.

*Table load alone* taken away, in the kernel with the new norm alone:

> The kernel before with the new second norm alone as changed (products 40 fold matmuls behind the sums), without the Sqrt table load put ahead. Theory: the first cast for the v group comes 1 to 3 us earlier than with it (782.6), but the scaling still starts at 773 or later, so most of the 2.5 us above before stays: 1 to 3 us above before. Rival (the casts alone decide): at or below before.

1286.41, ratio 1.0014 (1.0003 to 1.0025); scaling at 774.72, `x_b11h` at 782.05. The loss of 1.8 us lies within the expectation, and not clear of the 3.0 with the table load.

## Why the prediction was wrong

- *The norms on TensorE: right.* The sums take 0.58 us where they do not wait (0.7 forecast), and the products 1.05 by starts (0.95). With the waits out of the way `xb` starts 1.1 to 2.2 earlier than before; 2.1 was forecast. At the second norm the matmuls are as cheap, but against `qa_woa` TensorE comes to `qa_v` between 0.1 later and 2.1 earlier in the kernels with the norm as changed, since other waits differ from trace to trace. Four column groups do overlap; that rival falls. The change of tiling mode cost what the trace of before had shown (0.34 behind the sums), not a whole matmul.
- *The first fold: wrong in sign.* A gain of 0.3 was forecast, the halves cost 0.6: the head start is given back in waits for the second halves, and the sums wait for `ssq`.
- *The first stage's new waits: the wait right, its price wrong.* 2.5 us were called certain by the order, 2.6 came. The step that failed is the sum "-2.1 - 0.3 + 2.5 + 0.25 + 0.5 = +0.8": it has the length of the wait and nothing for the state in which it leaves TensorE. Behind it stands the premise that "the time can move in two ways only", fewer or cheaper matmuls or other waits; the runs showed a third, the same matmuls at half clock, which cost another 3.2 us. The price could be had from before: the last product of its trace, 1.19 for 0.68. `xb` came 5.3 late, with a bound of 1.7: 2.8 for the waits and 3.2 for the clock on a stage that would otherwise have been 1.1 early, and 0.4 that after's sums started later than those of that run. The products of the first norm did not wait.
- *Gates: the term was mis-sized, 0.3 forecast (0 to 1), 2.4 measured at `g`, though no run shows it in the time.* Two gates were priced at 1.2 each, and `uc` at 1.3 late; it came 2.9 late against `xb`. The step that failed is "a few tenths" for VectorE and GpSimd side by side, which was applied to the small instructions only. The rule of the Trainium skill ("GPSIMD Engine Reference", Key points) bears on a VectorE instruction with two inputs in the on-chip memory that both engines read, as a gate is, beside GpSimd's `wl_va`; the trace agrees with it, 3.40 for 1.22. Of before's trace `l` at 100.99 would have given the price. And the path was another: not `u` and the second `g`, but `uc`, the cast of `wh_xb` behind it on ScalarE, and `wl_xb`.
- *Decay constants: right.* 0.1 to 0.3 each (one 0.65), TensorE waits for none; GpSimd as a rival falls.
- *Second norm: -0.6 forecast (-2.1 to +1.4), +3.0 (1.5 to 4.5) measured alone.* The mechanism, VectorE without slack behind a late scaling, was right, as the held delay shows by its time. Two steps failed. One is "what is left of 2.1 is 2.1 - 1.5 = 0.6". By the prediction's own rows a split that comes 1.4 later, with 0.1 to spare, puts the matmul that reads it 1.3 later than before, however early TensorE gets there: the 2.1 cannot be set against it, and the term should have read +1.3, near the bound. The other is "I put it at 771.6", 1.8 later than before: in the kernel with the new norm alone it came at 773.67, 3.9 later. The 14 matmuls (3.2 us) by which the first product moves were right, but it started 3.3 later there (772.07 for 768.75), so hardly any of the gain had arrived by then. And the wait itself was not on `x_t1l` or `x_t2l`, neither in after nor with the new norm alone, but on ScalarE behind VectorE (`qb_v` 0.9 and `wq_g` 1.1 in after).
- *The rivals.* "The held queue" came nearest with 1290, by a wrong way: `vg` followed `xb` as before and no transfer held it up. "Both norms keep their gain" falls at the second norm.

Two things stay open. Gains made ahead of 130 us come out smaller in the time: both fixes together put `g` 9.1 us ahead of after and brought the loss against before from 5.5 us to 2.6, the gate behind put it 4.6 ahead (2.8 of that ahead of `xb`) and left the loss at 5.8. The traces put the difference behind 675 us, where the stretch from `qa_woa` to `fin_ms` takes 584 to 593 us from kernel to kernel and differs by 1.2 between two traces of the same one. Part of that is the clock: by the traces' records it falls again in this stretch in nine kernels (filler, two gates back, both weights early, old first fold, the two drawn together, the two early on both sides, table load alone), for 3.4 us in four, 6.8 in four and 13.7 in one. With half of that taken off, every stretch lies between 584.5 and 589.7, as those without a fall do. Why these still differ by 5 us was not found. And why the last fold's weights land later with the new second norm, table load or not, was not settled.

No version beats the kernel before by more than the runs can tell. The nearest is that with both fixes, the old second norm and the old first fold, 0.9998 (0.9983 to 1.0013).
